# A hybrid flow step on one core: X in one layout for both heads of a pair, and the affine steps of decay and rate on ScalarE

## The chip, the cores and the metric

The kernel runs on one core of a Trainium2 chip. The metric is the device time of one execution in microseconds. TensorE (PE in the profile; PEld is its weight loading), VectorE (DVE), ScalarE (ACT), GpSimd (POOL) and SyncE (SP, which here issues DMAs) run side by side, each through its own queue in order.

## The reference

One layer of a backbone for 128 context tokens and 512 latent tokens (640 columns in all, width 2048): RMSNorm with modulation, an input projection, a time mixer (RWKV-7, 16 heads of 64, forward and backward) beside a chunked gMLP, an output projection, and a SwiGLU channel mixer. The part around the change is the time mixer's preparation, for each direction d:

```
w_log = -softplus(-(w0[d] + tanh(wd) @ w2[d])) - 0.5
decay = exp(-exp(w_log))
a  = sigmoid(a0[d] + ad @ a2[d])
kd = k * (1 + (a - 1) * k_a)
y, s_fin = delta_scan(r, decay, kd, v, -kk, kk * a, s0[:, d], reverse=(d == 1))
# one step: sa = S a_t ;  S = S * w_t + sa b_t^T + v_t k_t^T ;  y_t = S r_t
```

## The kernel before, in words

**Stages.** The adaLN modulation and the norm come first (to some 210 us). Then a long stage (210 to 1110 us) runs the input projection and, in its gaps, prepares the time mixer. A stage of recurrence and output projection follows (about 1210 to 1530 us), then the channel mixer to the end.

**The main matmuls of the stage.** The output columns of the projection come in 43 blocks of 128 (`blocks`). For each block and each quarter of the 2048 inputs, `win` (L176) issues 24 matmuls of 320 columns in a high/low split of fp32: for each of two halves and four k-steps the lines L182, L183, L184. The weights come by `split` (L153): a DMA, a rounded copy on ACT (L160, `hi`) and the remainder on DVE (L161, `lo`). After the fourth quarter `take` (L919) copies the block out of PSUM (L924) and starts the generator that handles it.

**The planner.** Generators yield a cost at each step. `between` (L927) is called inside `win`, after the k-steps, and gives each of three `Mixer`s (L396) a budget; a mixer then runs its generators until the budget is spent. mixA holds the block handlers, mixS holds `solve`, mixM holds `merge`. `take` calls `mixA.finish(b - RAW)`, which runs at once all that is left of the handler of three blocks earlier. `take_k` is added with a declared cost KCOST = 35. The emitted instructions are then placed on their engines by the program builder, which can reorder independent ones; `chain` (L188) forces an order on PE.

**take_k (L520).** It runs once for each of the 8 pairs of heads (128 partitions, 64 for each head) and treats both directions. There are so 16 bodies, each over 640 columns, in 10 chunks of 64 (`v3` makes the chunk view, `rev` reverses time in a chunk for d = 1):

- L568, L571: low-rank products, then tanh on ACT gives `sg` (for the decay) and `tha` (for the rate a).
- L575: `sg` = 0.5 sg + 0.5, on DVE. L581: prefix sums of sg within the chunks, L. L584, L585: gam = exp(-c L) and L = exp(c L), on ACT.
- L592 to L598: R holds -kk times gam shifted by one step, and r times gam, side by side; L600 stores it. L604 loads v into Z.
- L606, L607: f = (kah tha + ka1) zk, the key after the rate, on DVE. L609: tha = -0.5 tha - 0.5, on POOL; L610: times nkk (that is -kk).
- L614 to L618: X holds f and tha, both times L, in four instructions of 64 partitions. In head 0 (partitions 0 to 63) part 0 of X is f and part 1 is tha; in head 1 it is the other way round.
- L629: for each chunk and head, the product of X (64 rows, 128 columns) with R (64 rows, 128 columns) into PSUM, both heads in separate banks, four chunks at a time. L635 copies one quarter of it (GB), L637 masks the half that is stored (GR, DMA at L640), L638 masks another quarter (GA).
- L645, L647, L649: X transposed on PE, copied on ACT into XT (two buffers) and stored in the record `d_S` with one DMA for each tile, in three tiles for a body (4, 4 and 2 chunks).
- L654: GA times the values into pW; L656 copies it into Z; L658 stores Z. L662: POOL issues eight DMAs of GB to DRAM for `solve`.

`solve` (L758) and `merge` (L786) invert the triangular blocks; all their DMAs are issued by POOL. The stage of recurrence loads the records of d_S (L1063). The modulation columns for later stages (L872, four groups of 32 columns of PE at a time) are also mixed in.

Of the kernel before, what the change touches and what calls it, by code (L numbers as in the profile page):

```python
# [13 lines left out]
AF = mybir.ActivationFunctionType  # L14
ALU = mybir.AluOpType
# [4 lines left out]
P = 128  # L20
# [5 lines left out]
CH = 64  # L26
# [55 lines left out]
F_R, F_G, F_X, F_Z, F_T, REC = 0, 128, 256, 384, 512, 576  # L82
# [3 lines left out]
def flow_step(ctx: ExitStack, tc, x_prompt, x_sample, state_rwkv, c, c_ctx, w_mod, b_mod,  # L86
# [3 lines left out]
    nc = tc.nc  # L90
    V, S, G, TE = nc.vector, nc.scalar, nc.gpsimd, nc.tensor
# [22 lines left out]
    for h in range(2):  # L114
        s = slice(CH * h, CH * h + CH)
# [5 lines left out]
                         op0=ALU.mult, op1=ALU.add)  # L121
# [24 lines left out]
    d_S = dp.tile([NPAIR, P, 2, NCH, REC], F32, name="d_S")  # L146
# [41 lines left out]
    def chain(made):  # L188

        for a, b in zip(made, made[1:]):  # L190
            tc.add_manual_dep(b.ins, a.ins.name, mybir.DependencyInfo(
                mybir.DependencyClass.NoSync, mybir.DependencyReason.DATA), reason="chain")
# [162 lines left out]
    v3 = lambda ap: ap.rearrange("p (c t) -> p c t", t=CH)  # L355
# [4 lines left out]
    hsl = lambda h: slice(64 * h, 64 * h + 64)  # L360
    osl = lambda h: slice(64 * (1 - h), 64 * (1 - h) + 64)
# [26 lines left out]
    kah = bk.tile([P, 8], F32, name="kah", bufs=1)  # L388
    V.tensor_scalar_mul(kah, prm[:, C_KA:C_KA + 8], 0.5)
    ka1 = bk.tile([P, 8], F32, name="ka1", bufs=1)  # L390
# [129 lines left out]
    def take_k(pr, p):  # L520
# [4 lines left out]
        def load_wl(d):  # L525

            raw = bk.tile([P, 2, P], F32, tag="GR", name="wlr", bufs=2)
            for h, w in enumerate((w2, a2)):
                nc.sync.dma_start(raw[:, h, :], w[0, d, :, p * P:(p + 1) * P].unsqueeze(0).to_broadcast([2, 64, P]))
            yield 0.5  # L530
            wh, wl = (bk.tile([P, 2, P], F32R, tag=n, name=n, bufs=1) for n in ("wh", "wl"))
            S.copy(wh, raw)
            V.tensor_sub(wl, raw, wh.bitcast(F32))
            o.wl = wh, wl
            yield 0.5
# [4 lines left out]
        nkk = bk.tile([P, T], F32, tag="nkk", name="nkk", bufs=1)  # L540
# [9 lines left out]
        for hf in range(2):  # L550
            s = slice(HALF * hf, HALF * hf + HALF)
# [5 lines left out]
        for d in range(2):  # L557
            rev = (lambda ap: ap[:, :, ::-1]) if d else (lambda ap: ap)
            last = 0 if d else CH - 1

            sg = bk.tile([P, T], F32, tag="t1", name="sg", bufs=2)
            tha = bp.tile([P, T], F32, tag="t3", name="tha", bufs=1)
            for hf in range(2):
                s = slice(HALF * hf, HALF * hf + HALF)
                two = [pk.tile([P, HALF], F32, tag=f"g{h}", name="pwa") for h in range(2)]
# [6 lines left out]
                yield 0.8  # L572
            if d == 0:
                yield from load_wl(1)
            V.tensor_scalar(sg, sg, 0.5, 0.5, op0=ALU.mult, op1=ALU.add)  # L575
            yield 0.4
            L = bp.tile([P, T], F32, tag="t2", name="L", bufs=1)
            for lo in (0, HALF):
                s = slice(lo, lo + HALF)
# [8 lines left out]
            n3, g3, i3 = v3(nkk), v3(gam), v3(L)  # L588
# [14 lines left out]
            for h in range(2):  # L603
                nc.sync.dma_start(Z[hsl(h), :, h, :], vsrc[:, :, hsl(h)])  # L604
            f = fs if d == 0 else bk.tile([P, T], F32, tag="t1", name="f", bufs=2)
            V.tensor_scalar(f, tha, kah[:, p:p + 1], ka1[:, p:p + 1], op0=ALU.mult, op1=ALU.add)  # L606
            V.tensor_mul(f, f, zk)  # L607
            yield 1.2
            G.tensor_scalar(tha, tha, -0.5, -0.5, op0=ALU.mult, op1=ALU.add)  # L609
            V.tensor_mul(tha, tha, nkk)  # L610
            yield 0.8

            X = bz.tile([P, NCH, 2, CH], F32, tag="X", name="X", bufs=1)
            V.tensor_mul(rev(X[0:64, :, 1, :]), v3(tha)[0:64], i3[0:64])  # L614
            V.tensor_mul(rev(X[64:128, :, 0, :]), v3(tha)[64:128], i3[64:128])
            yield 1.5
            V.tensor_mul(rev(X[0:64, :, 0, :]), v3(f)[0:64], i3[0:64])
            V.tensor_mul(rev(X[64:128, :, 1, :]), v3(f)[64:128], i3[64:128])  # L618
            yield 1.5
            if d == 1:  # L620
                V.tensor_add(fs, fs, f)
            n = 2 * p + d
# [3 lines left out]
            GA = bk.tile([P, NCH, CH], F32, tag="GA", name="GA")  # L626
            for (c0, c1) in ((0, 4), (4, 8), (8, NCH)):
                two = [pk.tile([P, 4, P], F32, tag=f"g{h}", name="pG") for h in range(2)]
                chain([TE.matmul(two[h][:, cc - c0, :], X[hsl(h), cc, :, :].rearrange("p s t -> p (s t)"),  # L629
                                 R[hsl(h), cc, :, :].rearrange("p s t -> p (s t)"), start=True, stop=True)  # L630
                       for cc in range(c0, c1) for h in (1, 0)])
                for h in range(2):
                    s, q, ps = hsl(h), osl(h), two[h]
                    mb = mask.unsqueeze(1).to_broadcast([P, c1 - c0, P])
                    S.copy(GB[q, c0:c1, :], ps[q, 0:c1 - c0, 0:CH])  # L635
                    GR = bk.tile([P, 4, CH], F32, tag="GR", name="GR", bufs=2)
                    V.tensor_tensor(out=GR[:, 0:c1 - c0, :], in0=ps[:, 0:c1 - c0, CH:P], in1=mb[:, :, CH:P], op=ALU.mult)  # L637
                    V.tensor_tensor(out=GA[s, c0:c1, :], in0=ps[s, 0:c1 - c0, 0:CH], in1=mb[s, :, 0:CH], op=ALU.mult)  # L638
                    yield 0.25 * (c1 - c0)
                    nc.sync.dma_start(d_S[p, :, d, c0:c1, F_G + CH * h:F_G + CH * h + CH], GR[:, 0:c1 - c0, :])  # L640

            for (c0, c1) in ((0, 4), (4, 8), (8, NCH)):
                ps = pk.tile([P, 4, P], F32, tag=f"g{c0 // 4 % 2}", name="pXT")
                for cc in range(c0, c1):
                    TE.transpose(ps[:, cc - c0, :], X[:, cc, :, :].rearrange("p s t -> p (s t)"), ident)  # L645
                XT = bz.tile([P, 4, P], F32, tag="XT", name="XT", bufs=2)
                S.copy(XT[:, 0:c1 - c0, :], ps[:, 0:c1 - c0, :])  # L647
                yield 0.2 * (c1 - c0)
                nc.sync.dma_start(d_S[p, :, d, c0:c1, F_X:F_X + P], XT[:, 0:c1 - c0, :])  # L649
            for c0 in (0, 5):  # L650
                ps = pk.tile([P, 5, CH], F32, tag=f"g{1 - c0 // 5}", name="pW0")
                for cc in range(c0, c0 + 5):
# [7 lines left out]
            for gq in range(8):  # L660
# [6 lines left out]
                               op0=ALU.mult, op1=ALU.mult)  # L667
# [230 lines left out]
    for p in range(NPAIR):  # L898
        block(P * p, take_r, 2.6, p)
        block(2 * DA + P * p, take_v, 5.1, p)  # L900
        block(DA + P * p, take_k, KCOST, p)
        while g < GORD[p]:
            block(CSH + DA + P * g, take_gv, 12.0, g)
            block(CSH + P * g, take_gu, 5.0, g)
            g += 1
# [112 lines left out]
    with ExitStack() as ph:  # L1018
# [17 lines left out]
        for k in (1, 3):  # L1036
            s = slice(32 * k, 32 * k + 32)
# [261 lines left out]
    X = {}  # L1299
# [61 lines left out]
    with ExitStack() as ph:  # L1361
# [7 lines left out]
                        in1=prm[:, C_N2:C_N2 + KB].unsqueeze(2).to_broadcast([P, KB, 2]), op=ALU.mult)  # L1369
# [13 lines left out]
        for hf in range(2):  # L1383
            s = slice(HALF * hf, HALF * hf + HALF)
# [502 lines left out]
    for t in range(NT):  # L1887
        for h in range(2):
            out = fin.tile([P, 4, 256], F32, tag=f"out{h}", name="out")
            src, f = (ap[:, 4 * h:4 * h + 4] for ap in (acc[:, :, t * 256:(t + 1) * 256], fg))  # L1890
# [36 lines left out]
```

## Time and profile before

| what | value |
|---|---|
| median of 3 runs | 3424.31 us (3414.05 to 3430.37) |
| the profiled execution | 3414.96 us, span 3413.2 us, mean granted PE clock 0.975 |
| PE busy | 3189.6 us (93%) |
| PEld busy | 2905.1 us (85%) |
| DVE busy | 2512.9 us (74%) |
| ACT busy | 1451.5 us (43%) |
| POOL busy | 1251.9 us (37%) |

Matmuls overlap each other, so PE's busy time counts the time in which at least one is under way. A group's line gives the source line, the engine, the operation, what it writes and reads, the shapes, the number of instructions, the busy time, the mean of one, and the time that the engine stood idle just before them with what ended the wait. A row of waits gives who waited for whom, the total, the number of times and the longest.

### The profile page before, as it was taken

What the parts mean: (1) busy time and instruction counts of PE and PEld (TensorE: products, weight loads), DVE (VectorE), ACT (ScalarE), POOL (GpSimd) and SP (SyncE); (2) the same over time, 40 slices, a digit from 0 to 9 for tenths busy, and PEclk for the clock granted to TensorE, in tenths of its full rate; (3) what the DMA queues carried; (4) which work ended last, traced back from release to release, by engine and by line L of the source; (5) the groups of instructions that cost most, each with busy time, mean ns of one, the idle gap of its engine ahead of it and who ended that gap; (6) DMA issues with size and microseconds to landing.
All of it is one profiled execution on the core that took longest, in us unless ns stands there. A gap on an engine that the chain in (4) does not pass through costs nothing.

```text
span 3413.2 us, 72346 instructions
## 1 busy us (share of the span) xinstructions
PE 3189.6 (93%) x28100; PEld 2905.1 (85%) x28100; DVE 2512.9 (74%) x4357; ACT 1451.5 (43%) x3172; POOL 1251.9 (37%) x1090
## 2 busy tenths in 40 slices
PE   6899989889988899989999999999999999999996
PEld 3688768768766877778999999999999999999986
DVE  4548577676766656656888888888878877877787
ACT  3334444444443433324644444444444444443365
POOL 0001121122112112321056565565666645555543
PEclk8999999999999899989999999999999999999998
DMA  8766676676767577735533434334343354543453
GB/s 322 242 191 200 194 195 175 168 204 180 198 185 193 149 221 238 219 112 158 171 113 115 125 105 126 120 110 124 112 123 113 116 178 141 153 148 114 146 165 115
DMA packets 719137, 552.94 MB, mean 162 GB/s; under 512 B 99449, under 2 KB 652425, under 8 KB 709961
## 3 DMA queue, kind: packets, MB, share of 16 engines
q1 hardware_dynamic: 706472, 534.61, 52.4%
q0 software_dynamic: 9984, 13.13, 2.0%
q8 instruction: 221, 3.62, 0.4%
q14 instruction: 124, 1.01, 0.1%
q10 hardware_dynamic: 2336, 0.57, 0.1%
HBM read 438.77 MB, written 111.69 MB: 161 GB/s over the span
## 4 chain that ended last, share of the span: by engine, by line
PE 50%; DVE 6%; issue 5%; DMA 3%; POOL 1%; ACT 1%; DVEq 0%; SPq 0%; ACTq 0%; POOLq 0%
PE P L1541 13%; PE P L1539 13%; PE P L1540 13%; DVE lo L1358 2%; PE big L1002 2%; DMA d_os<-act 1%; PE big L1003 1%; PE big L1004 1%; PE u_ps L1149 1%; PE y_ps L1105 1%; PE s_ps L1170 1%; PE pO L1217 1%; DVE act L1660 1%; PE big L1394 1%; PE big L1392 1%
## 5 line engine op out<-in xcount | busy, mean ns | idle before, releaser
L1541 PE MATMUL P<-xo,lo 128*128 128x320 f32 x2352 | 731.6, 311 | 11.1 <-DVE lo L1358 11.1
L1539 PE MATMUL P<-xo,hi 128*128 128x320 f32 x2352 | 728.2, 310 | 2.0 <-ACT hi L1357 2.0
L1540 PE MATMUL P<-xo,hi 128*128 128x320 f32 x2352 | 727.6, 309 | 0.0
L1358 DVE TENSOR_TENSOR lo<-raw,hi 128x512 fp32r<-128x512 f32 x532 | 585.9, 1120 | 64.1 <-ACT hi L1357 60.0
L1357 ACT CAST hi<-raw 128x512 fp32r<-128x512 f32 x532 | 326.4, 621 | 415.2 <-PE P L1540 320.4
L182 PE MATMUL big<-h_hi,hi 128*128 128x320 f32 x1376 | 452.1, 329 | 10.2 <-ACT h_hi L344 3.7
L1541 PEld LDWEIGHTS P<-xo,lo 128*128 128x128 f32 x2352 | 442.4, 188 | 18.9 <-DVE lo L1358 18.8
L1539 PEld LDWEIGHTS P<-xo,hi 128*128 128x128 f32 x2352 | 442.6, 188 | 2.9 <-ACT hi L1357 2.7
L1540 PEld LDWEIGHTS P<-xo,hi 128*128 128x128 f32 x2352 | 442.4, 188 | 0.0
L184 PE MATMUL big<-h_hi,lo 128*128 128x320 f32 x1376 | 436.6, 318 | 5.6 <-DVE lo L161 5.5
L183 PE MATMUL big<-h_lo,hi 128*128 128x320 f32 x1376 | 437.5, 318 | 0.5 <-DVE h_lo L345 0.5
L1452 POOL TENSOR_TENSOR raw<-raw 128x512 f32<-128x512 f32 x252 | 408.0, 1628 | 11.6 <-DVE lo L1358 1.6
L1541 PE MATMUL P<-xd,lo 128*128 128x320 f32 x1232 | 385.1, 313 | 17.8 <-DVE lo L1358 17.5
L1539 PE MATMUL P<-xd,hi 128*128 128x320 f32 x1232 | 383.7, 311 | 9.9 <-ACT hi L1357 6.8
L1540 PE MATMUL P<-xd,hi 128*128 128x320 f32 x1232 | 381.9, 310 | 0.0
L182 PEld LDWEIGHTS big<-h_hi,hi 128*128 128x128 f32 x1376 | 265.1, 193 | 76.8 <-issue 44.5
L161 DVE TENSOR_TENSOR lo<-raw,hi 128x512 fp32r<-128x512 f32 x268 | 185.7, 696 | 182.0 <-ACT hi L160 179.9
L160 ACT CAST hi<-raw 128x512 fp32r<-128x512 f32 x268 | 165.0, 618 | 295.1 <-PE big L183 122.2
L184 PEld LDWEIGHTS big<-h_hi,lo 128*128 128x128 f32 x1376 | 265.6, 193 | 12.7 <-DVE lo L161 7.4
L183 PEld LDWEIGHTS big<-h_lo,hi 128*128 128x128 f32 x1376 | 265.9, 193 | 7.9 <-issue 3.7
L1357 ACT CAST hi<-rawd 128x512 fp32r<-128x512 f32 (+1 forms) x288 | 168.7, 587 | 240.3 <-PE P L1540 222.6
L1452 POOL TENSOR_TENSOR t<-raw 128x512 f32<-128x512 f32 x84 | 135.8, 1617 | 343.1 <-DMA raw<-in_w_ffn_up_dram 325.7
(372 smaller groups left out, 6404.3 us busy)
## 6 DMA issues: line engine op xcount, KB each, us to landing
wt<-in_w_mod_dram SPq DMA_DIRECT2D x96, 1024.0 KB
raw<-in_w_ffn_gate_dram SPq DMA_DIRECT2D x182, 256.0 KB
raw<-in_w_ffn_up_dram SPq DMA_DIRECT2D x182, 256.0 KB
rec<-d_S SPq DMA_DIRECT2D x80, 576.0 KB
raw<-in_w_in_dram SPq DMA_DIRECT2D x172, 256.0 KB
rawd<-in_w_ffn_down_dram SPq DMA_DIRECT2D x128, 256.0 KB
raw<-in_w_out_dram SPq DMA_DIRECT2D x96, 256.0 KB
xd<-d_os SPq DMA_DIRECT2D x66, 320.0 KB
```

Of the source, the lines that this page charges most:

```text
L160: S.copy(hi, raw)
L161: V.tensor_sub(lo, raw, hi.bitcast(F32))
L182: TE.matmul(halves[hf], hi[:, k, :], h_hi[:, kb, s], start=(kb == 0), stop=False)
L183: TE.matmul(halves[hf], hi[:, k, :], h_lo[:, kb, s], start=False, stop=False)
L184: TE.matmul(halves[hf], lo[:, k, :], h_hi[:, kb, s], start=False, stop=(kb == KB - 1))
L1002: TE.matmul(halves[hf], hi[:, k, :], o_hi[kb][:, s], start=(k == 0), stop=False)
L1357: S.copy(hi[:, 0:nk], raw[:, 0:nk])
L1358: V.tensor_sub(lo[:, 0:nk], raw[:, 0:nk], hi[:, 0:nk].bitcast(F32))
L1452: G.tensor_tensor(out=o[:, 0:nk], in0=p[:, 0:nk], in1=q[:, 0:nk], op=ALU.subtract)
L1539: TE.matmul(ps, hi[:, k, :], xk[:, 0, :], start=f, stop=False)
L1540: TE.matmul(ps, hi[:, k, :], xk[:, 1, :], start=False, stop=False)
L1541: TE.matmul(ps, lo[:, k, :], xk[:, 0, :], start=False, stop=l)
```

## The change

Four things, all in `take_k`. The affine step of `sg` and the affine step of `f` move from DVE to ACT. The POOL step on tha goes; tha becomes (tha + 1) times nkk in one DVE instruction, and its factor -0.5 goes into the write of X. X has the same layout in both heads: part 0 is f, part 1 is tha, each written by one instruction of 128 partitions. The product with R is now two matmuls for each chunk and head, one for each part of X (64 rows, 64 columns), whose output partitions are chosen so that PSUM holds what it held before. Since the transposed X now has f in partitions 0 to 63 and tha in 64 to 127 for both heads, the store into d_S takes three DMAs: the columns of head 0 as they are, and the columns of head 1 in two halves, swapped. The yielded costs of the edited steps change, KCOST does not.

```diff
-            V.tensor_scalar(sg, sg, 0.5, 0.5, op0=ALU.mult, op1=ALU.add)
+            S.activation(sg, sg, AF.Copy, scale=0.5, bias=0.5)
             yield 0.4
...
-            V.tensor_scalar(f, tha, kah[:, p:p + 1], ka1[:, p:p + 1], op0=ALU.mult, op1=ALU.add)
+            S.activation(f, tha, AF.Identity, scale=kah[:, p:p + 1], bias=ka1[:, p:p + 1])
+            V.scalar_tensor_tensor(out=tha, in0=tha, scalar=1.0, in1=nkk, op0=ALU.add, op1=ALU.mult)
+            yield 0.8
             V.tensor_mul(f, f, zk)
-            yield 1.2
-            G.tensor_scalar(tha, tha, -0.5, -0.5, op0=ALU.mult, op1=ALU.add)
-            V.tensor_mul(tha, tha, nkk)
             yield 0.8
 
             X = bz.tile([P, NCH, 2, CH], F32, tag="X", name="X", bufs=1)
-            V.tensor_mul(rev(X[0:64, :, 1, :]), v3(tha)[0:64], i3[0:64])
-            V.tensor_mul(rev(X[64:128, :, 0, :]), v3(tha)[64:128], i3[64:128])
-            yield 1.5
-            V.tensor_mul(rev(X[0:64, :, 0, :]), v3(f)[0:64], i3[0:64])
-            V.tensor_mul(rev(X[64:128, :, 1, :]), v3(f)[64:128], i3[64:128])
-            yield 1.5
+            V.scalar_tensor_tensor(out=rev(X[:, :, 1, :]), in0=v3(tha), scalar=-0.5, in1=i3, op0=ALU.mult, op1=ALU.mult)
+            yield 0.8
+            V.tensor_mul(rev(X[:, :, 0, :]), v3(f), i3)
+            yield 0.8
...
-                chain([TE.matmul(two[h][:, cc - c0, :], X[hsl(h), cc, :, :].rearrange("p s t -> p (s t)"),
+                chain([TE.matmul(two[h][(osl if u else hsl)(h), cc - c0, :], X[hsl(h), cc, u, :],
                                  R[hsl(h), cc, :, :].rearrange("p s t -> p (s t)"), start=True, stop=True)
-                       for cc in range(c0, c1) for h in (1, 0)])
+                       for cc in range(c0, c1) for u in range(2) for h in (1, 0)])
...
-                nc.sync.dma_start(d_S[p, :, d, c0:c1, F_X:F_X + P], XT[:, 0:c1 - c0, :])
+                dst = d_S[p, :, d, c0:c1, F_X:F_X + P]
+                nc.sync.dma_start(dst[:, :, 0:CH], XT[:, 0:c1 - c0, 0:CH])
+                for h in range(2):
+                    nc.sync.dma_start(dst[hsl(h), :, CH:P], XT[osl(h), 0:c1 - c0, CH:P])
```

`hsl(h)` is the 64 partitions of head h, `osl(h)` those of the other head.

## The prediction

> **What bounds the kernel now.** I read the page first, then a table of busy time by stage, then the waits of PE inside the stage that the edit touches, and last the groups and the timeline of the edited lines. On the page, these two rows of the 40 slices (85.3 us each) matter:
>
> ```profile
> PE   6899989889988899989999999999999999999996
> DVE  4548577676766656656888888888878877877787
> ```
>
> The edit is in `take_k`, whose instructions run from 210 to 1110 us (slices 3 to 13). PE shows 8 or 9 there, DVE 5 to 8. By stage (length, then PE, PEld, DVE, ACT, POOL busy with counts, granted clock, DMA share, GB/s):
>
> ```profile
> 210.00:1110.00 900.00, 815.61 (x9401) 677.02 (x9400) 628.24 (x1276) 393.18 (x854) 180.35 (x288) 0.98 0.70 190
> 1110.00:1210.00 100.00, 89.71 (x1065) 84.35 (x1063) 64.81 (x120) 38.95 (x77) 13.12 (x18) 0.91 0.57 157
> 1210.00:1530.00 320.00, 307.80 (x4526) 245.30 (x4525) 206.57 (x669) 108.83 (x496) 85.46 (x112) 0.97 0.67 199
> 1530.00:3413.00 1883.00, 1806.51 (x12058) 1777.00 (x12056) 1514.15 (x2051) 840.94 (x1632) 966.64 (x653) 0.99 0.43 131
> ```
>
> In the stage PE is busy 91%, DVE 70%, ACT 44%. What follows 1210 us runs none of the edited lines and reads the same records, so the change is worth what it does to these 900 us and no more. There PE works through the input projection in a fixed order, and `take_k`'s small products are slotted in between. So the time that can be won is not DVE's 628 us but the time in which PE stood still for DVE. The waits of PE in this stage (total us, times, longest):
>
> ```profile
> PE pG L629 <- DVE X L618: 11.5, 10, 4.0
> PE pG L629 <- DVE GA L638: 10.8, 18, 1.9
> PE psp L740 <- DVE vt L727: 7.6, 3, 3.2
> PE pwa L568 <- DVE wl L533: 7.1, 2, 3.7
> ...
> PE pXT L645 <- DVE GA L638: 5.9, 6, 3.2
> PE big L184 <- DVE lo L161: 4.8, 3, 4.3
> ...
> PE pwa L568 <- DVE mx L774: 4.1, 1, 4.1
> PE pvt L703 <- DVE praw L684: 3.1, 5, 1.0
> ```
>
> Only the first row is the edited chain: ten times in the sixteen (pair, direction) bodies PE waited for the last write of X, 11.5 us in all. That is 0.3% of the run. The other seven rows are other DVE work, 43.4 us.
>
> **The change part by part: DVE.** The groups (busy us, mean ns | idle before):
>
> ```profile
> L575 DVE TENSOR_SCALAR sg<-sg 128x640 f32<-128x640 f32 x16 | 7.8, 490 | 52.7 <-ACT sg L571 52.7
> L606 DVE TENSOR_SCALAR f<-tha,kah,ka 128x640 f32<-128x640 f32 x8 | 4.9, 611 | 0.2
> L607 DVE TENSOR_TENSOR f<-f,zk 128x640 f32<-128x640 f32 x8 | 6.6, 819 | 0.1
> L609 POOL TENSOR_SCALAR tha<-tha 128x640 f32<-128x640 f32 x16 | 22.3, 1395 | 206.5 <-DVE fs L606 153.7 <-ACT gam L584 32.8 <-DVE f L606 19.9
> L610 DVE TENSOR_TENSOR tha<-tha,nkk 128x640 f32<-128x640 f32 x16 | 13.0, 815 | 2.5 <-POOL tha L609 2.5
> L614 DVE TENSOR_TENSOR X<-tha,L 64x640 f32<-64x640 f32 x16 | 12.9, 807 | 0.0
> L615 DVE TENSOR_TENSOR X<-tha,L 64x640 f32<-64x640 f32 x16 | 13.2, 822 | 0.3
> L617 DVE TENSOR_TENSOR X<-f,L 64x640 f32<-64x640 f32 x8 | 6.5, 809 | 0.0
> L618 DVE TENSOR_TENSOR X<-f,L 64x640 f32<-64x640 f32 x8 | 6.5, 817 | 0.0
> L684 DVE SCALAR_TENSOR_TENSOR praw<-gq,praw 128x640 f32<-128x640 f32 x11 | 9.0, 817 | 1.0 <-ACT gq L682 1.0
> L584 ACT ACTIVATE gam<-L 128x640 f32<-128x640 f32 x16 | 11.8, 740 | 21.8 <-DVE L L581 21.8
> ```
>
> Before, one body costs DVE 0.490 + 0.611 + 0.819 + 0.815 + 0.807 + 0.822 + 0.809 + 0.817 = 5.99 us. The X writes on 64 partitions cost what the 128-partition products beside them cost (0.807 to 0.822 against 0.815), so each pair of half writes becomes one instruction of 0.82. After, DVE has f times zk (0.82), the fused (tha+1)*nkk (0.817, the fused form's row L684) and two X writes (2 x 0.82): 3.28 us. DVE loses 2.71 us a body, 16 x 2.71 = 43.4 us: 628 becomes 585 of 900.
>
> How much of it reaches PE? At most the 11.5 us of the first wait row if the order on PE stays. But that order was made ahead by a builder that places an instruction where its operands are due by its own reckoning; if X is reckoned earlier, the products move forward on PE and meet a later X again. The trace cannot show which; I take half, -6 (bounds -11.5 and 0). For the other seven rows, a DVE that is 7% less busy takes perhaps a tenth off 43.4 us: -4 (bounds -14, a third, and 0).
>
> **POOL.** L609's 22.3 us leave POOL, and its 206.5 us of standing in the queue go with it; behind it POOL issues the DMAs of `solve` and `merge`. On DVE the POOL step cost only the 2.5 us of L610's row. No PE wait row names POOL: 0.
>
> **ACT.** Two activations of 128x640 come in, at 0.740 each (row L584): 16 x 1.48 = 23.7 us, 393 becomes 417 of 900. They replace two DVE steps in a chain that already starts with ACT's tanh, so the affine of the rate follows its producer on the same engine. What is new is a wait: the fused product overwrites tha in place, so DVE must wait until ACT has read tha for f. ACT sometimes stands:
>
> ```profile
> ACT hi L160 <- PE big L183: 88.2, 52, 5.8
> ```
>
> An affine step queued behind such a cast waits 88.2/52 = 1.7 us on average. Behind the fused product stand, on DVE, both X writes and the `lo` subtractions that feed the main matmuls. In most bodies the scan and R (L581 to L598) lie between, so I charge +1 (bounds 0 and 16 x 1.7 = 27).
>
> **PE.** The product inside a chunk was one 64-row by 128-column matmul per head; now it is two with 64 columns each, over the same 128 streamed columns. The records double, 640 to 1280. How such products overlap is seen in the timeline (start, duration, merged count):
>
> ```profile
> 232.21 1.04 PE L872 MATMUL pm<-wt,cT 128*2 128x512 f32 x8 [0.49 <-DMA wt<-in_w_mod_dram]
> 233.18 0.41 PE L183 MATMUL big<-h_lo,hi 128*128 128x320 f32 x1
> ...
> 236.31 1.16 PE L629 MATMUL pG<-R,X 64*128 64x128 f32 x16
> 237.40 0.42 PE L182 MATMUL big<-h_hi,hi 128*128 128x320 f32 x1
> ...
> 247.89 0.72 PE L629 MATMUL pG<-R,X 64*128 64x128 f32 x8
> 248.53 0.42 PE L184 MATMUL big<-h_hi,lo 128*128 128x320 f32 x1
> ...
> 296.57 1.05 PE L740 MATMUL psp<-wspT,vt 128*128 128x128 f32 x8
> 297.38 0.39 PE L182 MATMUL big<-h_hi,hi 128*128 128x320 f32 x1
> ```
>
> Sixteen records hold PE for 237.40 - 236.31 = 1.09 us, eight for 248.53 - 247.89 = 0.64; eight more cost 0.45 us, 56 ns a record. The same 128 columns over the whole array (L740) cost 0.81 us for eight, 101 ns a record. So the two heads' products, on different rows, run side by side. The L872 row shows that products on the same rows and different columns do so as well: eight records of 512 columns take 0.97 us where one after the other they would take 8 x 4 x 0.101 = 3.2. The new form has both: two row halves times two column halves. If all four run together, 32 records still take the 1.09 us and the cost is only the longer start of each of the 48 bursts. I take +3 (0.06 us a burst, about one record). If only two run at a time, 640 more records at 56 ns: +36. The bounds are 0 and +36, and the L872 row, the only one with shared rows, puts it near the low end.
>
> The Trainium skill, page "TensorE: Matmul & The Clock Gate", Part 3, says that a weight load overlaps running matmuls only when its row group differs. The two halves of one head share a row group, so by that rule they would take turns, and the sum would end at the high price. Its Part 1 also lets a load into the background weight buffer be pulled ahead, and the L872 row speaks for that.
>
> **The store of X.** Each XT tile went out with one DMA and now with three: 48 become 144.
>
> ```profile
> L649 SPq DMA_DIRECT2D d_S<-XT x48: 359/367/2154, 251.4 to 1083.0; - x48
> ...
> L647 ACT COPY XT<-pXT 128x512 f32<-128x512 f32 (+1 forms) x48 | 24.1, 515 | 24.0 <-PE pXT L645 16.0 <-DMA d_S<-XT 7.5 <-DMA d_S<-GR 0.2
> ...
>   ACT XT L647: 8.8, 18
> ```
>
> SP takes 0.367 us to issue one, so 96 more are 35 us of SP's 900, and every load queued behind an XT tile issues 0.73 us later. There are two XT buffers and three tiles per body: the third copy waits until the first tile's DMAs have landed (the 7.5 us in ACT's row), and the last row, from the waits of the products into pW (L654), shows that PE already stood 8.8 us for XT copies. With the landing 0.73 us later in 16 bodies it is 12 us at most; in about a fifth it will be PE's last wait: +2 (bounds 0 and +12). The bytes are the same, in rows of half the length; with the DMA engines 0.70 busy in the stage I charge nothing for that.
>
> **The planner.** The yields of the edited steps fall from 5.0 to 3.2 units a direction; `take_k` keeps its declared 35, which is under its real sum (51.8 before, 48.2 after). Walking the generators through the planner, direction 1 of every pair is emitted in one lump when a later block forces `take_k` to finish, in both versions at the same block. Only direction 0's products are emitted earlier, by 8 groups of three main matmuls, in five of the eight pairs. I cost that at 0: it only changes which main matmuls stand before them and which behind.
>
> **Sum.** -6 - 4 + 0 + 1 + 3 + 2 = -4 us on the profiled execution's 3414.96 (span 3413.2 and 1.8 around it): 3411. The median of the runs is 3424.31, 9.4 higher, so for the median I forecast 3420. The three runs spread over 16 us; 0.5%, or 17 us, is about what a measurement of this kernel can tell from no change, and the forecast lies inside it.
>
> **The rivals.**
> - Relief of DVE: the order on PE keeps up, all 11.5 us of X waits go and a third of the other 43.4 (14.5). That is -26, or 3398. For it: X came last ten times. Against it: PE's work itself is unchanged and 91% busy.
> - Quadrants in pairs (slower): the four products of a chunk take turns two by two, +36 in place of +3. With the rest of the sum it is +29, or 3453. It decides when the span of 32 records exceeds about 1.6 us; at 2.0 us it is all there. Against it: the L872 row.
> - ACT in the way (slower): f sits behind casts that wait for PE, 16 x 1.7 = 27 in place of +1, so +22, or 3446. It needs that wait to be the last one in nearly every body.
> - The change does nothing that shows, because the builder packs PE as tightly as before: 3424. That lies with the forecast.
>
> **How the numbers follow.** Chances: forecast with the null case 0.50 (its own range 3407 to 3441), relief 0.28, quadrants in pairs 0.15, ACT in the way 0.07. The range runs from just under relief, 3396, to the pairs case, 3453. Faster by over 0.5% 0.28, within it 0.50, slower 0.22.
>
> **What would show it.** Right: DVE's busy time in the stage falls by some 44 us, ACT's rises by 24, a burst of 32 product records lasts about 1.1 to 1.2 us, waits of pG for X fall below 8 us, and the stage stays within 15 us of its length. Wrong: bursts of 2 us; a new wait of DVE for ACT's f of over 15 us; PE's waits for XT above 15 us; or the waits of PE for DVE halved as a whole, with the main matmuls closer together.

## The result and the profile after

| | before | after |
|---|---|---|
| median of 18 runs each | 3419.05 us (3407.28 to 3430.37) | 3408.49 us (3402.81 to 3418.16) |
| ratio to before | 1 | 0.9977, 95% interval 0.9968 to 0.9986 |
| span of the profiled execution | 3413.2 us | 3401.0 us |

By the ratio the change is worth 0.23%, some 8 us (5 to 11), which is inside the 0.5% band. The two medians differ by 10.6 us; the runs below are compared by the ratio and its interval.

The stage of the edit in the changed kernel (length, then PE, PEld, DVE, ACT, POOL busy with counts, granted clock, DMA share, GB/s):

```profile
210.00:1110.00 900.00, 820.89 (x10089) 681.37 (x10089) 590.23 (x1224) 416.12 (x889) 157.70 (x272) 0.96 0.72 190
```

DVE's busy time fell by 38.0 us, ACT's rose by 22.9, POOL's fell by 22.7. The granted clock, the share of its full clock that TensorE was given, is 0.96 here and was 0.98 before. The edited lines as groups (busy us, mean ns | idle before):

```profile
L626 PE MATMUL pG<-R,X 64*64 64x128 f32 x1280 | 51.3, 295 | 25.4 <-DVE GA L635 12.6 <-DVE X L615 9.5 <-ACT hi L160 3.3
...
L613 DVE SCALAR_TENSOR_TENSOR X<-tha,L 128x640 f32<-128x640 f32 x16 | 13.1, 816 | 0.0
L607 DVE SCALAR_TENSOR_TENSOR tha<-tha,nkk 128x640 f32<-128x640 f32 x16 | 13.0, 811 | 0.0
L575 ACT ACTIVATE sg<-sg 128x640 f32<-128x640 f32 x16 | 11.9, 743 | 0.2
L606 ACT ACTIVATE fs<-tha,ka,kah 128x640 f32<-128x640 f32 x8 | 7.4, 923 | 0.0
```

How far the stage came is seen from the last main matmul. These are L182's rows (min/median/max ns, first and last start in us), before and after:

```profile
L182 PE MATMUL big<-h_hi,hi x1376: 303/308/935, 53.4 to 1163.0; 128*128 128x320 f32 x197
```

```profile
L182 PE MATMUL big<-h_hi,hi x1376: 303/308/935, 53.1 to 1156.6; 128*128 128x320 f32 x197
```

The stage ends 6.4 us earlier. The remaining 5.8 of the two profiles' 12.2 us arise later, where no edited line runs, and the runs of the changed kernel spread over 15 us, those of the kernel before over 23. From 210 us up to that last main matmul the stage reads, before and after:

```profile
210.00:1162.80 952.80, 864.65 (x10142) 723.37 (x10141) 660.56 (x1330) 414.50 (x894) 190.93 (x303) 0.97 0.69 186
```

```profile
210.00:1156.50 946.50, 860.89 (x10776) 718.71 (x10776) 616.96 (x1267) 435.42 (x924) 168.30 (x287) 0.96 0.71 187
```

PE stood still for 88.2 us of it before (952.80 - 864.65) and for 85.6 after. The waits of PE in the stage of the changed kernel (total us, times, longest):

```profile
PE pG L626 <- DVE GA L635: 12.6, 15, 2.5
PE pm L872 <- DMA wt<-in_w_mod_dram: 11.9, 8, 3.8
PE pG L626 <- DVE X L615: 9.5, 6, 8.3
```

Two things stand out against the rows of before. The wait for X is one single wait of 8.3 us and five that come to 1.2 us. And PE's wait for the DMA of modulation weights has gone up to 11.9 us; before, its row was:

```profile
PE pm L872 <- DMA wt<-in_w_mod_dram: 6.7, 8, 1.7
```

The single wait of 8.3 us, in the last body, can be followed back in the timeline:

```profile
1046.68 0.37 ACT L644 COPY XT<-pXT 128x256 f32<-128x256 f32 x1 [1.71 <-DMA d_S<-XT]
1048.59 0.80 PE L654 MATMUL pW<-Z,GA 64*64 64x64 f32 x20
...
1050.34 0.42 PE L568 MATMUL pwa<-waM,wh 128*128 128x320 f32 x1 [0.95 <-ACT Z L656]
...
1052.68 0.74 ACT L575 ACTIVATE sg<-sg 128x640 f32<-128x640 f32 x1
1053.45 1.54 DVE L581 TENSOR_TENSOR_SCAN L<-scan,sg 128x320 f32<-128x320 bf16 x2 [9.59 <-ACT sg L575]
...
1059.46 0.82 DVE L615 TENSOR_TENSOR X<-f,L 128x640 f32<-128x640 f32 x1
```

The third copy of XT waits 1.71 us for a store of X, which by the two buffers is that of the first tile. The products into pW come after it, and the copies of Z, the low-rank products, the tanh, the scan and X follow one another from there, while DVE stands 9.59 us. PE did not stand before the products into pW, though, so how much of the 8.3 us the 1.71 us brought is not shown. The wait points at the stores, and so do the weights: ACT's casts wait longer for their loads (first row before, second after):

```profile
ACT hi L160 <- DMA raw<-in_w_in_dram: 16.4, 8, 3.9
```

```profile
ACT hi L160 <- DMA raw<-in_w_in_dram: 42.9, 19, 7.8
```

### The profile page after: what moved, and what is told of

Same layout as the page of the kernel before. It is cut to its first block, busy times and chain, and to the rows that moved or that the text cites. A ratio compares the mean times of both kernels' runs of the same rounds, so it can differ in the third digit from the quotient of the medians.

```text
span 3401.0 us, 73675 instructions
## 1 busy us (share of the span) xinstructions
PE 3177.1 (93%) x28740; PEld 2893.7 (85%) x28740; DVE 2472.6 (73%) x4293; ACT 1473.8 (43%) x3204; POOL 1230.1 (36%) x1074
## 4 chain that ended last, share of the span: by engine, by line
PE 57%; DVE 9%; issue 6%; DMA 5%; ACT 2%; POOL 1%; SPq 0%; DVEq 0%; ACTq 0%; POOLq 0%
PE P L1541 13%; PE P L1539 13%; PE P L1540 13%; DVE lo L1358 2%; PE big L1002 2%; DMA d_os<-act 2%; PE big L182 1%; PE big L183 1%; PE big L184 1%; PE big L1003 1%; PE big L1004 1%; DVE act L1660 1%; PE pm L872 1%; PE u_ps L1149 1%; PE y_ps L1105 1%
## 5 line engine op out<-in xcount | busy, mean ns | idle before, releaser
L182 PE MATMUL big<-h_hi,hi 128*128 128x320 f32 x1376 | 452.6, 329 | 12.9 <-ACT hi L160 6.7
L1452 POOL TENSOR_TENSOR raw<-raw 128x512 f32<-128x512 f32 x252 | 408.6, 1631 | 11.6 <-DVE lo L1358 1.6
L182 PEld LDWEIGHTS big<-h_hi,hi 128*128 128x128 f32 x1376 | 265.2, 193 | 76.0 <-issue 41.3
```

Source lines behind the costliest of these rows:

```text
L182: TE.matmul(halves[hf], hi[:, k, :], h_hi[:, kb, s], start=(kb == 0), stop=False)
L1452: G.tensor_tensor(out=o[:, 0:nk], in0=p[:, 0:nk], in1=q[:, 0:nk], op=ALU.subtract)
```

## The experiments

The theory: the gain is DVE's relief and the three stores take part of it back. The rivals: POOL's place in the chain is what mattered; or the gain is a matter of order, of where the builder puts the products. All ratios are to the kernel before in the same session, five rounds each.

**The affine half alone.** On the kernel before:

```diff
-            V.tensor_scalar(sg, sg, 0.5, 0.5, ...)
+            S.activation(sg, sg, AF.Copy, scale=0.5, bias=0.5)
...
-            V.tensor_scalar(f, tha, ...)  ...  G.tensor_scalar(tha, ...) ; V.tensor_mul(tha, tha, nkk)
+            S.activation(f, tha, AF.Identity, ...) ; V.scalar_tensor_tensor(out=tha, ...)
...
-            V.tensor_mul(rev(X[0:64, :, 1, :]), v3(tha)[0:64], i3[0:64])      # and the other half
+            V.scalar_tensor_tensor(out=rev(X[0:64, :, 1, :]), ..., scalar=-0.5, ...)
```

> The affine steps on ACT, the fused step on DVE and no POOL step, with X written in the old layout by four half instructions, one product for each head and one store. DVE gives up 0.49 + 0.61 us a body, 18 of the 38 us that the whole change took from its busy time in the stage. Theory (PE's waits shrink with DVE's work, whatever part it comes from): about half of the gain of 0.23%, a ratio to before of 0.9985 to 0.9992. Rival (POOL's place in the chain was what mattered): all of the gain, 0.998 or less. Rival (ACT in the way): 1.000 or more, with DVE waiting for f.

Measured: 0.9987 (0.9976 to 0.9998), 4.4 us. That is what the theory gave; with POOL out of the chain as well it did not bring the whole. It is less than what a change of order alone moves (see the old yields below), so it is not shown to be DVE's relief.

**The layout half alone.** The changed kernel with the old lines for sg, f and tha (and tha written into X without the factor).

> X in one layout, two writes of 128 partitions, products by quadrants and three stores, while the affine steps stay on DVE and the POOL step stays in the chain. DVE gives up 1.64 us a body, 26 us. Theory (PE's waits shrink with DVE's work): somewhat over half of the gain, 0.998 to 0.999. Rival (POOL mattered): 1.000. Rival (the three stores cost what the writes save): 1.000 or more, with longer waits of ACT for the XT stores and of PE for XT.

Measured: 0.9971 (0.9956 to 0.9986), 10 us, with three stores. It is as good as the whole change: what the affine half gave alone is not added to it.

**One store.** On the changed kernel:

```diff
-                dst = d_S[p, :, d, c0:c1, F_X:F_X + P]
-                nc.sync.dma_start(dst[:, :, 0:CH], ...)                            # and two half stores
+                nc.sync.dma_start(d_S[p, :, d, c0:c1, F_X:F_X + P], XT[:, 0:c1 - c0, :])
```

> The changed kernel, with one DMA for each XT tile as before the change; the halves of head 1 are left unswapped in the record, so the recurrence computes on another order of rows. Theory (the three stores cost PE a few us, as the 8.3 us wait of the last body in the changed kernel suggests, where ACT waited 1.7 us for a store): 2 to 8 us faster than the changed kernel, 0.9955 to 0.997 of before, and the wait of PE in the last body gone. Rival (the stores are hidden; that wait has another cause): as the changed kernel, 0.9977 within 0.001.

Measured: 0.9905 (0.9886 to 0.9924), median 3380.16: 25 us below the changed kernel, three times the most that was expected. The stage ends at 1130.8, and the recurrence, which alone reads the other order of rows, comes only after that:

```profile
L182 PE MATMUL big<-h_hi,hi x1376: 303/308/637, 53.0 to 1130.8; 128*128 128x320 f32 x197
```

PE's waits for the modulation weights, and ACT's for the projection's weights, are back where they were before the change, and the wait for X is small:

```profile
PE pm L869 <- DMA wt<-in_w_mod_dram: 6.4, 7, 1.9
```

```profile
ACT hi L160 <- DMA raw<-in_w_in_dram: 17.9, 6, 9.0
...
PE pG L626 <- DVE X L615: 2.8, 5, 1.2
```

Up to the last main matmul PE stood still for 62.5 us (920.70 - 858.17), where it was 85.6 in the changed kernel:

```profile
210.00:1130.70 920.70, 858.17 (x10776) 714.74 (x10775) 616.82 (x1267) 435.70 (x924) 168.38 (x287) 0.97 0.70 192
```

The stores are not all that differs, though. There are 48 bursts of products pG (three for each body). Counted by the main matmuls ahead of them on PE, 26 of the 48 stand elsewhere than in the changed kernel, 23 of them earlier, by up to 24 main matmuls: with other stores the builder made another order.

**The old yields.** On the changed kernel, at the four edited steps:

```diff
-  yield 0.8 ; yield 0.8 ; yield 0.8 ; yield 0.8
+  yield 1.2 ; yield 0.8 ; yield 1.5 ; yield 1.5
```

> The changed kernel with the old yields (1.2, 0.8, 1.5, 1.5) at the edited steps, so that the planner emits as before the change. Theory (the planner's yields cost nothing): as the changed kernel, 0.9977 within 0.001. Rival (the gain is one of order: where the products of direction 0 stand): moved by over 0.0015 from the changed kernel.

Measured: 0.9998 (0.9986 to 1.0011). The whole gain of 0.23% goes with it, though no operation differs. So order alone moves some 7 us, and a single comparison below that size settles nothing here. On PE 12 of the 48 bursts stand later than in the changed kernel, by 6 to 24 main matmuls, all of them in two of the eight pairs.

**Three stores on the kernel before.**

```diff
-                nc.sync.dma_start(d_S[p, :, d, c0:c1, F_X:F_X + P], XT[:, 0:c1 - c0, :])
+                nc.sync.dma_start(dst[:, :, 0:CH], XT[:, 0:c1 - c0, 0:CH])
+                for h in range(2):
+                    nc.sync.dma_start(dst[hsl(h), :, CH:P], XT[hsl(h), 0:c1 - c0, CH:P])
```

> The kernel before, with nothing changed but the store of each XT tile: three DMAs of the same bytes (one of 64 columns over all partitions, two of 64 columns over half of them, to where they belong), so 96 more issues on SP and rows of 256 bytes. Theory A (the stores are what holds the gain back, by late weight loads behind them on SP): 15 to 30 us slower than before, ratio 1.004 to 1.009, with ACT's wait for the weight DMAs (16.4 us before) above 30. Theory B (the 26 us by which the one-store run beat the changed kernel are mostly a luckier order): 1.000 to 1.002.

Measured: 1.0031 (1.0015 to 1.0048), 10.6 us slower, between the two theories. The stores cost without anything else of the change; ACT's wait for weights went to 34.1 us, from 16.4.

```profile
ACT hi L160 <- DMA raw<-in_w_in_dram: 34.1, 17, 7.8
```

That wait is not shown to be the way in which they cost. Up to its last main matmul the stage took 11.6 us longer than in the kernel before, but PE stood still only 1.2 us more (89.3 against 88.2); its busy time grew by 10.4:

```profile
210.00:1174.40 964.40, 875.06 (x10151) 731.78 (x10150) 667.58 (x1334) 414.28 (x897) 194.93 (x303) 0.96 0.70 184
```

The granted clock was lower, by the mean over whole runs 0.972 in the 9 runs of this kernel against 0.975 in the 22 of the kernel before beside them. And 27 of the 48 bursts stand elsewhere on PE, 19 of them later.

**The layout half with one store.** The layout half of above with the store of the one-store run.

> The layout half of the change alone (two X writes, products by quadrants; affine steps and the POOL step as before the change), with one store; the halves of head 1 are left unswapped in the record. Theory A (the stores cost 20 us or more): 20 us or more below the layout half with three stores, ratio to before 0.990 to 0.993. Theory B: 0.996 to 0.9985, as with three.

Measured: 0.9913 (0.9898 to 0.9929). That is 20 us below the same kernel with three stores, and 30 us below the kernel before. With the affine half on top it is 0.9905: with one store the affine half is worth nothing that can be told.

**The three stores from ACT's queue.** `nc.sync` becomes `nc.scalar` in the three lines.

> The changed kernel with the three stores of each tile issued from ACT's queue in place of SP's. Same packets and same bytes. If SP's queue is where the stores cost (weight loads behind a store that waits, or behind its issue time): ratio 0.991 to 0.995, ACT's wait for weight DMAs back at 15 to 25 us. If the small packets on the DMA engines cost: as the changed kernel, 0.9977 or more. If issuing costs ACT as much: 0.998 or more with ACT's copies late.

Measured: 1.0038 (1.0023 to 1.0053), worse than from SP. The copies into XT now wait for stores that stand in the same queue:

```profile
ACT XT L644 <- DMA d_S<-XT: 41.4, 14, 5.7
```

ACT's wait for weights, 29.9 us, did not come back to 15 to 25 either. So this run did not tell what it was made for: one cost left SP and another came to ACT.

**The swap on PE.** On the changed kernel:

```diff
-  TE.transpose(ps[:, cc - c0, :], X[:, cc, :, :]..., ident)
+  for u in range(2):
+      for h in range(2):
+          TE.matmul(two[h][(osl if h else hsl)(u), cc - c0, :], X[hsl(h), cc, u, :], I2[hsl(h), :], ...)
...
+  S.copy(XT[:, 0:c1 - c0, CH * h:CH * h + CH], two[h][:, 0:c1 - c0, :])    # for each h, then one store
```

> The changed kernel with the swap of head 1 done on PE: X is turned by four 64x64 products with the identity for each chunk, into two banks, two copies of 64 columns into XT, and one store as before the change. ACT copies 96 tiles of half the columns (at some 0.35 us) in place of 48, +9 us on ACT. Theory A: most of what one store gave, 0.991 to 0.995. Theory B: 0.997 to 0.999.

Measured: 1.0027 (1.0015 to 1.0039); both expectations failed. Four chunks take longer on PE, as the timelines show (the kernel before first, then this one):

```profile
250.11 0.60 PE L645 MATMUL pXT<-ident,X 128*128 128x128 f32 x4
250.46 0.39 PE L182 MATMUL big<-h_hi,hi 128*128 128x320 f32 x1
```

```profile
255.33 1.13 PE L644 MATMUL pXT<-I,X 64*64 64x64 f32 x32
256.39 0.62 PE L182 MATMUL big<-h_hi,hi 128*128 128x320 f32 x1
```

From first start to the next main matmul that is 0.35 us before and 1.06 here. But the granted clock was 0.50 from 255.3 to 256.4 us of this run, and 1.00 at the place shown for the kernel before. The main matmuls just ahead of this burst, at 0.50 too, start 0.27 us apart, those from 257.0 us on, at the full clock, 0.15. Taken at the full clock alone, 17 bursts of 32 records last 0.63 to 1.29 us, 0.89 in the median, and 16 bursts of four before 0.35 to 0.61, 0.47 in the median. With 40 times four chunks in the stage, that is by estimate 17 us of PE, a good part of what one store gives.

**Three stores of full rows.** The one-store variant, cut by partitions:

```diff
+                for s in (slice(0, 64), slice(64, 96), slice(96, 128)):
+                    nc.sync.dma_start(dst[s], XT[s, 0:c1 - c0, :])
```

> The one-store variant of the changed kernel with its store cut in three by partitions (64, 32 and 32), so three issues a tile as in the changed kernel, but rows of 512 bytes as in the one-store run; the halves of head 1 are left unswapped. If the number of issues on SP costs the 25 us: as the changed kernel, 0.996 to 0.999 of before. If the 256-byte rows cost: as with one store, 0.989 to 0.992.

Measured: 0.9982 (0.9970 to 0.9994), as the changed kernel. So the row length does not matter; three DMAs for a tile in place of one do. On PE all 48 bursts stand behind the same main matmul as in the changed kernel, unlike those of the one-store run, so this run does not tell how much of the cost is the issuing itself and how much the order that the builder made around it. The wait rows are those of the changed kernel too, down to the 8.3 us in one body:

```profile
PE pm L871 <- DMA wt<-in_w_mod_dram: 13.1, 9, 3.8
...
PE pG L626 <- DVE X L615: 9.1, 4, 8.3
```

**The swap in ACT's copies.** On the changed kernel, with one store:

```diff
-                S.copy(XT[:, 0:c1 - c0, :], ps[:, 0:c1 - c0, :])
+                S.copy(XT[:, 0:c1 - c0, 0:CH], ps[:, 0:c1 - c0, 0:CH])
+                for h in range(2):
+                    S.copy(XT[hsl(h), 0:c1 - c0, CH:P], ps[osl(h), 0:c1 - c0, CH:P])
```

> The changed kernel with the swap done by ACT: three copies out of PSUM for each tile (64 columns as they are, and two of 64 partitions into the other half), one store of 512-byte rows. ACT works some 24 us more in the stage (96 more copies of about 0.25 to 0.37 us less what the shorter ones save), PE no more than the changed kernel. If the stores were the cost and ACT has room: 0.991 to 0.995. If ACT's copies on the way to the next products count as much: 0.997 to 1.000.

Measured: 0.9942 (0.9928 to 0.9956), median 3397.18. It beats both kernels: 20 us below the kernel before and, by the ratios, 12 us below the changed one. The copies cost ACT 23.7 us more than L644's 24.1 in the changed kernel, and PE's wait for X is down from 9.5 to 2.3 us:

```profile
L646 ACT COPY XT<-pXT 64x256 f32<-64x256 f32 (+1 forms) x96 | 31.8, 331 | 1.1
...
L644 ACT COPY XT<-pXT 128x256 f32<-128x256 f32 (+1 forms) x48 | 16.0, 334 | 20.7 <-PE pXT L642 17.4 <-DMA d_S<-XT 2.9
```

```profile
PE pG L626 <- DVE X L615: 2.3, 6, 0.6
```

**One of the copies on DVE.** `V.tensor_copy` for the copy of h = 1.

> As the run before with one of the two half copies on DVE, which has 38 us of room in the stage since the change. If the chain of copies counts: 2 to 6 us faster than with all three on ACT. If DVE's queue is the later one: 2 to 6 us slower.

Measured: 0.9989 (0.9977 to 1.0001), 16 us slower than with all three on ACT, well beyond what either answer allowed. The weight waits stay low (18.3 us for ACT's casts), so late weights are not all that moves the stage.

```profile
ACT hi L160 <- DMA raw<-in_w_in_dram: 18.3, 11, 3.7
```

What moved it here is PE's busy time. Up to the last main matmul the stage is 13.1 us longer than with all three copies on ACT, and PE is busy for 12.0 of them, on the same products (that run first):

```profile
210.00:1146.90 936.90, 864.31 (x10783) 719.27 (x10783) 616.70 (x1268) 461.06 (x1022) 167.69 (x287) 0.97 0.70 189
```

```profile
210.00:1160.00 950.00, 876.27 (x10797) 729.61 (x10796) 633.21 (x1316) 447.28 (x975) 168.38 (x287) 0.96 0.69 186
```

The mean granted clock of its 12 runs was 0.971, of the 6 runs with three copies on ACT 0.976. If PE set the pace throughout, that is an estimate of 17 us (0.5% of 3400). So these 16 us go mostly with a lower clock; what lowered it is not shown.

**The layout half with the swap in the copies.** The same copies and one store; sg, f and tha as before the change.

> The layout half alone with the swap in ACT's copies and one store: two X writes, products by quadrants, three copies a tile; both affine steps stay on DVE and the POOL step stays. ACT is relieved of the 16 x (0.74 + 0.91) us of the affine steps, DVE has 18 us more. If the affine half of the change is worth nothing once the stores are gone (as the two one-store runs, 0.9905 and 0.9913, say): 0.993 to 0.996. If ACT, which now has the copies too, was the later one: 0.990 to 0.993. If DVE was: 0.996 to 0.999.

Measured: 0.9940 (0.9919 to 0.9961), median 3397.96: the same as with the affine half. Twice, then, the affine half added nothing to the layout half with one store.

## Why the prediction was right, point by point

The time came out inside the forecast band, 8 us down where 4 were forecast, but the terms of the sum did not: a larger gain and a larger cost cancelled, so the number was in part luck. Of the signs named beforehand the wait of pG for X failed: 9.5 us, where under 8 was to show that the account was right.

- **DVE's saving**: 43.4 us forecast, 38.0 measured in the same window, which holds a little more of the stage now, and 43.6 (660.56 - 616.96) up to the last main matmul of each. The prices by instruction were right: the fused step 811 ns against 817, each X write 816 against 820.
- **What reaches PE**: -6 and -4 forecast. The two runs with one store are 30 and 32 us below the kernel before (0.9913 and 0.9905 of some 3413), the size of the relief rival (-26). Summed over the stage up to its last main matmul, the waits of PE that a DVE instruction ended went from 61 us to 37 in the changed kernel and 36 with one store. Its other waits went from 26 to 47 us in the changed kernel and stayed at 25 with one store. So the waits for DVE fell by 24 us and not by 10 already with three stores, and other waits took their place. Not all of that shift is relief: with the three stores alone on the kernel before, where DVE has its old work, the two sums are 45 and 43, so in part only another instruction came last. And the one-store runs have another order on PE.
- **PE's products**: +3 forecast, in truth a little below zero. In the changed kernel 32 records hold PE for 234.02 - 232.99 = 1.03 us where 16 took 1.09, and so in all 24 such bursts at the full clock:

```profile
232.99 1.10 PE L626 MATMUL pG<-R,X 64*64 64x128 f32 x32
234.02 0.41 PE L182 MATMUL big<-h_hi,hi 128*128 128x320 f32 x1
```

  All four quadrants ran together; the rival of quadrants in pairs is out, and so is, for this form, the rule of the Trainium skill ("TensorE: Matmul & The Clock Gate", Part 3) that the second half of a head would wait with its weight load. What the prediction sets against it, a load into the background weight buffer, stands in Parts 2 and 3 of that page of the Trainium skill, not in Part 1; the 1.03 us fit it.
- **The store of X**: +2 forecast, with bounds 0 and +12. This is the step that failed. Measured it is 10.6 us on the kernel before, 20 on the layout half and 25 on the whole. The number of issues was right, their length was not: a store of all 128 partitions holds SP for 0.366 us, as priced, but each of the two of 64 partitions for 0.607:

```profile
L649 SPq DMA_DIRECT2D d_S<-XT x96: 580/607/1812, 248.8 to 1083.3; - x96
```

  A tile holds SP 1.21 us longer (0.366 + 2 x 0.607 - 0.367) and not 0.73, the 48 tiles 58 us and not 35. And what stands behind them on SP was priced only for XT itself; the loads of weights stand there too, and ACT's wait for them went from 16.4 to 42.9 us. That three DMAs a tile cost, whatever their rows, is shown by the run with three full rows. By which way they cost stays open. PE's waits for X and for the modulation weights together are 12 us shorter with one store. But in each of the three pairs of kernels that differ in the number of stores alone, 26 or 27 of the 48 bursts stand elsewhere on PE, and where the stores alone were added the time went with PE's busy time at a lower clock.
- **ACT**: +1 forecast. The affine step of sg took 743 ns, as priced, but that of f took 906 to 923, not 740; no wait of DVE for f shows among its rows, so the rival of ACT in the way did not come about. The affine half is worth 4.4 us on the old kernel and nothing on the better ones.
- **POOL**: 0 forecast; no run separated POOL's step from the affine steps, and the two together gave 4.4 us at most.
- **The planner**: 0 forecast. The old yields cost the whole gain. That is a move of order, which the walk through the planner saw (the products of direction 0 in five pairs; on PE it is both directions of two pairs) and priced at nothing.
- **The granted clock**: no term of the sum. The means of the kernels' runs lie between 0.970 (the stores from ACT's queue) and 0.978 (the layout half with one store), and 0.001 is an estimate of up to 3.4 us of 3400. So a part of the differences above goes with the clock. No run holds it fixed, and what sets it here stays open.

## What to carry to other kernels

Count the issues of a queue and read how long each takes, not only the bytes: two more DMAs a tile on a queue that also feeds the main loop cost 10 to 25 us here, up to three times what the whole change gained. When a change moves the time little, take its parts away one by one; here a gain of 30 us lay under a cost of 20 to 25. And where a builder sets the order, measure a change of order alone before believing a difference of its size, and compare PE's busy time and the granted clock before looking for the missing time among the waits.

## What the runs showed of the hardware that was not expected

- In four 64x64 quadrants a record of 128 columns costs 27 ns (32 records 1.03 us, and 16 of them 245.20 - 244.60 = 0.60 us; 0.43 us for 16 more), half of the 56 ns that it cost in two row halves. With only 64 columns to stream (the swap on PE), 17 bursts of 32 records at the full clock took 0.63 to 1.29 us, 0.89 in the median, so half the columns did not halve the time.

```profile
244.60 0.67 PE L626 MATMUL pG<-R,X 64*64 64x128 f32 x16
245.20 0.42 PE L182 MATMUL big<-h_hi,hi 128*128 128x320 f32 x1
```

- An activation of 128x640 with scale and bias read for each partition takes 0.91 to 0.92 us, with constants 0.74.
- ACT copies 64 partitions of PSUM into the other half of the partitions at 331 ns on average, the same as 128 partitions of the same length without a move (334).
- Three stores a tile of 256-byte rows and three of 512-byte rows took the same time (0.9977 and 0.9982 of the kernel before).
- A store of 64 partitions holds SP longer than one of 128: 0.607 us for rows of 256 bytes, 0.596 for rows of 512 (the run with three full rows), against 0.366.
